# Ten of eleven gate and up pairs of each feed-forward as Strassen groups instead of nine

## The chip, the cores and the metric

The kernel runs on one core of one Trainium2 chip. The metric is device time of one execution in microseconds (us), the median of the runs shown. Lower is better. The core's engines are named as in the profile: PE (TensorE, matmuls), PEld (its weight loads), DVE (VectorE), ACT (ScalarE), POOL (GpSimd) and SP (SyncE, which issues most of the DMAs). Each engine has its own list of instructions and takes them in that order.

## The reference

One encoder block in float32 on 256 rows of width 2048: a SwiGLU feed-forward, two token mixers (band attention and retention) merged by gates, a second SwiGLU feed-forward, and a final norm. Only the two feed-forwards are touched by the change:

```python
D_MODEL = 2048; SEQ = 256; D_FF = 5632
def swiglu_ffn(x, w_gate, w_up, w_down):
    return (jax.nn.silu(x @ w_gate) * (x @ w_up)) @ w_down
...
x = x + 0.5 * swiglu_ffn(rmsnorm(x, norm_ffn1_g[l]), ffn1_w_gate[l], ffn1_w_up[l], ffn1_w_down[l])
... # mixers
x = x + 0.5 * swiglu_ffn(rmsnorm(x, norm_ffn2_g[l]), ffn2_w_gate[l], ffn2_w_up[l], ffn2_w_down[l])
```

`w_gate` and `w_up` are 2048 x 5632, `w_down` is 5632 x 2048. All weights are read from HBM once per use; the 256 rows of activations stay on chip as two tiles of 128 rows (t = 0, 1).

## The kernel before, in words

**Arithmetic.** Float32 precision comes from splitting every operand into a rounded part `hi` and a rest `lo`, and from three products, hi·hi, lo·hi and hi·lo (`three`, lines 132, 133 and 135: activations' hi and lo with the weights' hi, then activations' hi with the weights' lo). Weights arrive in chunks of 256 rows by 512 columns, as a tile of 128 x 1024 elements. Each chunk is split on the chip: ACT writes `hi` (line 123), then DVE writes `lo` = raw - hi (line 124). The products run as matmuls of 128 x 512.

**Steps.** The program is a list of steps, and a step is the work on one split chunk.
- A *standard step* (`standard`) is one chunk of an ordinary matmul job (`Gemm`): 2 k-tiles x 2 row tiles x 3 products = 12 matmuls. Its chunk comes through SP into one of five raw buffers. On DVE it costs one split.
- A *group step* (`Strassen.step`) belongs to a gate and up pair of 512 columns computed as a Strassen group: seven half-size products instead of eight. It has 6 matmuls, on the two row tiles or a combination of them. A group has 28 of them in four phases: phases 0, 1 and 2 have eight each (four "r" steps on a weight block as it is and four "s" steps on a running sum, in pairs "rr", "sr", "sr", "ss"), phase 3 has four "s" steps. Each has a split. DVE also forms the sums of weight blocks: four additions in phase 0 (line 515), eight in phase 1 (lines 570 and 557), all on 128 x 1024 elements. The blocks that stay for the sums (tiles named k and x) come through POOL's queue, and a third block is added to x by four DMAs that accumulate (line 558).
- At the end of a group, DVE has two rescalings (line 745), one combination each at lines 619 and 630, and two splits of the finished product into the operand of `down` (line 364), six instructions on 128 x 512 in all; PE has eight transposes for it (line 369). ACT reads the group's accumulators at the ends of phases (lines 610, 613, 616 and 627). All accumulations of phases 1 to 3 that go on in accumulator "a" wait for that read.

Two numbers make up a group's name in the trace: `z128` is the group that begins at step 128, `loz12833s` is the lo tile of its phase 3, chunk 3, an "s" step. Split tiles of standard steps are plain `hi` and `lo`.

**What runs ahead.** There are four pairs of hi and lo buffers (`SPLIT_BUFS`): before the products of step c are issued, the splits up to step c + 3 are (`prep_upto`), so the split of step c + 4 begins when PE has done with step c.

**The order of a feed-forward.** Of the eleven column blocks of gate and up, nine are Strassen groups and two (`PLAIN`, blocks 9 and 10) are pairs of standard jobs, 8 + 8 standard steps each. `down` is done in seven passes over one or two blocks (`PASSES`), each pass four jobs of 2 standard steps per block; a pass reads x from the residual into the accumulator (line 762) and writes it back (line 765). `weave` puts all standard steps, in the order of a list of jobs, between the group steps. Twelve go first (`LEAD`), the last 14 stay for the end, and the others are dealt out by a credit that grows with each pair of group steps:

```python
job, k = queue[0]
if any(at_hand.get(b, len(steps) + 1) > len(steps) for b in job.needs):
    return False
...
rate = (len(queue) - apart) / (len(groups) * sum(SHARE))
...
    steps.extend(part)
    credit += rate * SHARE[i]
    if i + 1 == len(SHARE):
        at_hand[b] = len(steps) + 7
    turn = i + 1 == 3 * (HALF_K // KC)
    if (turn or credit >= (0.2 if (i + 1) % (HALF_K // KC) == 0 else 0.6)) and next_standard():
        credit -= 1
```

`SHARE` gives 0.85 per pair in phase 0, 1.0 in phase 1, 0.8 and three times 0.4 in phase 2, and 0.15 for each step of phase 3; it sums to 10. A standard step of a `down` pass is only placed once every block that the pass needs is `at_hand`, seven steps after that block's group has ended; until then none is placed, whatever the credit. `turn` asks for one between phases 2 and 3. The lines are those of `weave`; it is called by `ffn`, which the change edits, and by the mixers' projections, which it doesn't touch.

Of the kernel before, what the change touches and what calls it, by code (L numbers as in the profile page):

```python
# [41 lines left out]
HELD = 6  # L42

SHARE = (0.85,) * 4 + (1.0,) * 4 + (0.8,) + (0.4,) * 3 + (0.15,) * 4
PLAIN = (9, 10)
PASSES = ((9, 0), (1, 2), (10, 3), (4, 5), (6,), (7,), (8,))
GATE_WAIT = 5
WARM = (6, 3)
TAIL_PARTS = ((0, slice(0, NB)), (1, slice(0, NB // 2)), (1, slice(NB // 2, NB)))
# [23 lines left out]
def block_kernel(ctx: ExitStack, tc: tile.TileContext, x, g1, w1g, w1u, w1d, gm, w_in, rel, woa, wor, wo,  # L73
# [21 lines left out]
    def tmp_tile(name, tag="t", bufs=None):  # L95
        return tmp.tile([P, NB], F32, tag=tag, name=name, bufs=bufs)
# [9 lines left out]
    def later(n, fn):  # L106
        due.setdefault(state["step"] + n, []).append(fn)
# [529 lines left out]
    def down_done(b, factor, after):  # L637
        def done(acc):
            for t in range(NT):
                xb = xs[t][:, b * NB : (b + 1) * NB]  # L640
                nc.vector.scalar_tensor_tensor(xb, acc[t], factor, xb, op0=ALU.mult, op1=ALU.add)
            if after is not None:
                after(b)

        return done
# [11 lines left out]
    def weave(jobs, apart, groups, lead, start=None):  # L657


        queue = [(job, k) for job in jobs for k in range(0, job.nk, KC)]  # L660
        at_hand = {}

        def next_standard():

            if len(queue) <= apart:
# [4 lines that stand above are left out]
            steps.append(standard(job, k))  # L670
            del queue[0]
            if job.makes is not None and k + KC == job.nk:
                at_hand[job.makes] = len(steps) + 6
            return True

        for _ in range(lead):
            next_standard()
        rate = (len(queue) - apart) / (len(groups) * sum(SHARE))
        credit = 0.0
        first = len(steps) - 8  # L680
        for n, (b, make) in enumerate(groups.items()):
            group = make()
            loads = group.loads()
            if start is not None and n == 0:
                loads[0] = lambda load=loads[0]: [start(), load()]
            kept.extend((first + i if n == 0 else 0, fn) for i, fn in enumerate(loads))
            for i, part in enumerate(group.steps()):
# [8 lines that stand above are left out]
        for job, k in queue:  # L696
            steps.append(standard(job, k))

    def ffn(name, norm, wg, wu, wd, after, start=None):


        nblocks = DFF // NB
        mids, ready = {}, {}

        def put_mid(b, hs):
            mids[b] = Operand(f"{name}a{b}", 1)
            for t in range(NT):
                mids[b].put(0, t, hs[t])

        def plain(b):  # L710
            gates = {}

            wait = GATE_WAIT if start is not None and b == PLAIN[0] else 0

            def gate_done(acc):
                def go():
                    for t in range(NT):
                        gates[t] = tmp_tile(f"{name}g{b}{t}", "gate", 2)
                        nc.scalar.activation(gates[t], acc[t], AF.Silu, scale=norm.scale(t))

                if wait:
                    later(wait, go)
                else:
                    go()

            def up_done(acc):
                for t in range(NT):
                    a = gates[t]
                    nc.vector.scalar_tensor_tensor(a, acc[t], norm.scale(t), a, op0=ALU.mult, op1=ALU.mult)  # L729
                later(4, lambda: put_mid(b, gates))  # L730

            tags = ("acc", "acc")
            up = Gemm(wu, 0, b * NB, D // P, norm, up_done, tags)
            up.makes = b
            return [Gemm(wg, 0, b * NB, D // P, norm, gate_done, ("z", "z") if wait else tags), up]

        def paired(b):
            got = {}

            def evict(t, side, r):  # L740
                if side == 1:
                    nc.scalar.activation(r, r, AF.Silu)
                    got[t] = r
                    return
                nc.vector.scalar_tensor_tensor(got[t], r, norm.scale(t), got[t], op0=ALU.mult, op1=ALU.mult)
                if t == 1:
                    later(4, lambda: put_mid(b, got))

            return Strassen(norm, wu, b * NB, wg, b * NB, evict)

        def down(blocks, last):

            jobs = []

            def act(k, t):
                return mids[blocks[k // 4]](k % 4, t)

            for b in range(D // NB):
                cols = slice(b * NB, (b + 1) * NB)

                def seed(acc, t, cols=cols):
                    nc.scalar.activation(acc, xs[t][:, cols], AF.Copy, scale=2.0)  # L762

                def evict(acc, t, cols=cols):
                    nc.scalar.activation(xs[t][:, cols], acc, AF.Copy, scale=0.5)  # L765

                if last:
                    job = Gemm(wd, 0, b * NB, 4 * len(blocks), act, down_done(b, 0.5, after))
                else:
                    job = Gemm(wd, 0, b * NB, 4 * len(blocks), act, None, ("acc", "acc"), seed)  # L770
                    job.evict = evict
                job.rows = [(m * 4 + i) * P for m in blocks for i in range(4)]
                job.needs = blocks
                jobs.append(job)
            return jobs

        downs = {blocks: down(blocks, blocks is PASSES[-1]) for blocks in PASSES}
        first, second = [plain(b) for b in PLAIN]
        order = [first, second[:1], downs[PASSES[0]], second[1:]] + [downs[p] for p in PASSES[1:]]
        jobs = [job for part in order for job in part]  # L780
        for job, follow in zip(jobs, jobs[1:]):
            job.next = follow
        groups = {b: (lambda b=b: paired(b)) for b in range(nblocks) if b not in PLAIN}
        weave(jobs, len(downs[PASSES[-1]]) * len(PASSES[-1]) * 4 // KC + HELD, groups, LEAD, start)

# [5 lines left out]
    def third_block():  # L791

        there = small.tile([P, NB // P], F32, tag="there", name="there", bufs=1)
        nc.gpsimd.tensor_tensor(there, n1.raw[2][:, 0, : NB // P], mhalf, op=ALU.mult)

    ffn("f1", n1, w1g[0], w1u[0], w1d[0], x_updated(nm), third_block)


# [291 lines left out]
    def tail_done(acc, t, cols):  # L1090
# [24 lines left out]
        for src, dst in ((xs[t][:, c0:c1], slice(c0, c1)), (end, slice(c1, D))):  # L1115
            nc.scalar.activation(src, src, AF.Copy, scale=rs)
            nc.sync.dma_start(out[0, rows, dst], src)
            if dst.start == c0:
                nc.sync.dma_start(out[0, rows, :c0], xs[t][:, :c0])

    ffn("f2", n2, w2g[0], w2u[0], w2d[0], last_block)


# [125 lines left out]
```

## Time and profile before

| | before |
|---|---|
| median of 3 runs | 2069.69 us (2069.14 to 2071.16) |
| profiled execution: its own time | 2071.38 us |
| profiled execution: span of the trace | 2069.5 us |
| PE busy | 2048.4 us (99%), 9256 matmuls |
| PEld busy | 1694.7 us (82%) |
| DVE busy | 1756.4 us (85%), 1825 instructions |
| ACT busy | 1405.0 us (68%), 1734 instructions |
| POOL busy | 273.6 us (13%) |
| moved by DMA | 473.28 MB, mean 229 GB/s |

Starts in the trace count from the span's begin. The first feed-forward fills the first 704 us or so, the second one those from 1377 us on. Matmuls overlap in the pipeline, so the time that one takes from PE is the distance between two starts, not its duration; the same holds for DVE, whose instructions in a row overlap a little. An idle time in brackets stands before the instruction that it precedes, with what ended it.

### The profile page before, as it was taken

The numbers are of one execution on the slowest core, as the hardware profiler recorded it, in microseconds if no ns is written. First come the engines' busy times: TensorE is split into PE (matmuls) and PEld (weight loads), VectorE is DVE, ScalarE is ACT, GpSimd is POOL, SyncE is SP. The second block draws the span as 40 slices with busy tenths as digits, with TensorE's granted clock in tenths as the row PEclk, the third lists the DMA queues.
The fourth block names the chain that finished last, engine by engine and source line by source line (L and its number), as shares of the span: only waits on it lengthen the run. The fifth ranks groups of instructions, "written<-read, shape, count | busy, mean of one in ns | idle before, by whom it ended". The sixth has DMA issues, their size and how long they took to land.

```text
span 2069.5 us, 26149 instructions
## 1 busy us (share of the span) xinstructions
PE 2048.4 (99%) x9256; PEld 1694.7 (82%) x9256; DVE 1756.4 (85%) x1825; ACT 1405.0 (68%) x1734; POOL 273.6 (13%) x322
## 2 busy tenths in 40 slices
PE   9999999999999999999999999999999999999998
PEld 7788888888887888888888888888888888888886
DVE  7998999898997799899966667568989988998986
ACT  8677667777777767776765434556776677677785
POOL 1111211122111110122100000010122012110200
PEclk9999999999999999999999999999999999999999
DMA  8776887788668677898775645575797668876873
GB/s 306 204 227 223 274 227 207 238 264 260 191 230 262 212 205 257 260 289 251 226 268 174 220 134 194 185 238 175 240 275 233 200 224 272 242 206 232 275 214 132
DMA packets 219027, 473.28 MB, mean 229 GB/s; under 512 B 14784, under 2 KB 15536, under 8 KB 218896
## 3 DMA queue, kind: packets, MB, share of 16 engines
q1 hardware_dynamic: 161088, 310.42, 44.7%
q0 software_dynamic: 54752, 155.88, 27.9%
q10 hardware_dynamic: 3056, 5.32, 0.7%
q8 instruction: 72, 1.18, 0.2%
q14 instruction: 59, 0.48, 0.1%
HBM read 462.65 MB, written 8.91 MB: 228 GB/s over the span
## 4 chain that ended last, share of the span: by engine, by line
PE 94%; DVE 2%; DMA 1%; ACT 1%; issue 1%; ACTq 0%; POOLq 0%; POOL 0%; DVEq 0%
PE acc L135 17%; PE acc L132 17%; PE acc L133 17%; DMA raw<-in_ffn_w_down_dram 1%; DVE lo L124 1%; ACT hi L123 1%; PE z684a L135 0%; PE z51a L132 0%; PE z380a L135 0%; PE z51a L133 0%; PE z166a L133 0%; PE z128a L132 0%; PE z380a L132 0%; PE z418a L132 0%; PE z761a L133 0%
## 5 line engine op out<-in xcount | busy, mean ns | idle before, releaser
L124 DVE TENSOR_TENSOR lo<-raw,hi 128x1024 fp32r<-128x1024 f32 (+1 forms) x401 | 487.8, 1220 | 182.1 <-ACT hi L123 177.5
L123 ACT CAST hi<-raw 128x1024 fp32r<-128x1024 f32 (+1 forms) x401 | 418.6, 1048 | 227.9 <-PE acc L133 147.3
L765 ACT ACTIVATE xall<-acc 128x512 f32<-128x512 f32 x96 | 56.6, 589 | 9.6 <-PE acc L135 7.7
L762 ACT ACTIVATE acc<-xall 128x512 f32<-128x512 f32 x96 | 57.5, 599 | 7.5 <-DVE f1g L729 3.1
L132 PE MATMUL acc<-hi,mgh 128*128 128x512 f32 x128 | 50.2, 392 | 0.0
L133 PE MATMUL acc<-hi,mgl 128*128 128x512 f32 x128 | 49.8, 389 | 0.0
L132 PE MATMUL acc<-hi,nma01h 128*128 128x512 f32 x96 | 38.7, 403 | 0.0
L132 PE MATMUL acc<-hi,nma00h 128*128 128x512 f32 x96 | 38.6, 402 | 0.0
L133 PE MATMUL acc<-hi,nma00l 128*128 128x512 f32 x96 | 37.5, 391 | 0.0
L133 PE MATMUL acc<-hi,nma01l 128*128 128x512 f32 x96 | 37.5, 390 | 0.0
L132 PE MATMUL acc<-hi,nma10h 128*128 128x512 f32 x96 | 37.5, 390 | 0.0
L133 PE MATMUL acc<-hi,nma11l 128*128 128x512 f32 x96 | 37.4, 390 | 0.0
L133 PE MATMUL acc<-hi,nma10l 128*128 128x512 f32 x96 | 37.4, 390 | 0.0
L132 PE MATMUL acc<-hi,nma11h 128*128 128x512 f32 x96 | 37.4, 390 | 0.0
L135 PE MATMUL acc<-lo,mgh 128*128 128x512 f32 x128 | 35.6, 390 | 0.0
L135 PE MATMUL acc<-lo,nma00h 128*128 128x512 f32 x96 | 29.6, 390 | 0.0
L135 PE MATMUL acc<-lo,nma11h 128*128 128x512 f32 x96 | 29.6, 390 | 0.0
L135 PE MATMUL acc<-lo,nma01h 128*128 128x512 f32 x96 | 29.6, 390 | 0.0
L135 PE MATMUL acc<-lo,nma10h 128*128 128x512 f32 x96 | 29.6, 390 | 0.0
L135 PEld LDWEIGHTS acc<-lo,mgh 128*128 128x128 f32 x128 | 24.0, 188 | 5.0
L133 PEld LDWEIGHTS acc<-hi,mgl 128*128 128x128 f32 x128 | 24.1, 188 | 4.8
L132 PEld LDWEIGHTS acc<-hi,mgh 128*128 128x128 f32 x128 | 24.0, 188 | 4.9
(6130 smaller groups left out, 6938.3 us busy)
## 6 DMA issues: line engine op xcount, KB each, us to landing
raw<-in_ffn_w_down_dram SPq DMA_DIRECT2D x176, 512.0 KB, 6.0
raw<-in_w_in_dram SPq DMA_DIRECT2D x96, 512.0 KB, 4.7
raw<-in_ffn_w_up_dram SPq DMA_DIRECT2D x32, 512.0 KB, 10.1
raw<-in_w_out_dram SPq DMA_DIRECT2D x32, 512.0 KB, 3.9
raw<-in_ffn_w_gate_dram SPq DMA_DIRECT2D x31, 512.0 KB, 6.0
raw<-in_w_out_att_dram SPq DMA_DIRECT2D x16, 512.0 KB, 4.2
raw<-in_w_out_ret_dram SPq DMA_DIRECT2D x16, 512.0 KB, 4.0
z380x<-in_w_in_dram POOLq DMA_DIRECT2D x8, 512.0 KB, 7.8
```

Source lines behind the costliest of these rows:

```text
L123: nc.scalar.copy(hi[:, p, :], raw[:, p, :])
L124: nc.vector.tensor_sub(lo[:, p, :], raw[:, p, :], hi[:, p, :].bitcast(F32))
L132: nc.tensor.matmul(acc, ahi, whi, start=first, stop=False, **more)
L133: nc.tensor.matmul(acc, alo, whi, start=False, stop=False, **more)
L135: nc.tensor.matmul(acc, ahi, wlo, start=False, stop=last, **more)
L762: nc.scalar.activation(acc, xs[t][:, cols], AF.Copy, scale=2.0)
L765: nc.scalar.activation(xs[t][:, cols], acc, AF.Copy, scale=0.5)
```

## The change

One of the two standard pairs of each feed-forward becomes a Strassen group, so there are ten groups and one standard pair (block 9). The passes of `down` are dealt anew: block 9 alone has the first pass, then come four pairs of blocks, and blocks 8 and 10 have a pass each. The list of standard jobs is now block 9's gate and up, then all passes.

```diff
-PLAIN = (9, 10)
-PASSES = ((9, 0), (1, 2), (10, 3), (4, 5), (6,), (7,), (8,))
+PLAIN = (9,)
+PASSES = ((9,), (0, 1), (2, 3), (4, 5), (6, 7), (8,), (10,))
...
         downs = {blocks: down(blocks, blocks is PASSES[-1]) for blocks in PASSES}
-        first, second = [plain(b) for b in PLAIN]
-        order = [first, second[:1], downs[PASSES[0]], second[1:]] + [downs[p] for p in PASSES[1:]]
+        order = [plain(b) for b in PLAIN] + [downs[p] for p in PASSES]
         jobs = [job for part in order for job in part]
```

By the lists of both programs, counted over both feed-forwards, PE has 48 matmuls of 128 x 512 less; DVE has 24 splits more, 8 more of each of the additions at lines 515, 557 and 570, and 4 small instructions more; ACT has 24 copies at line 123 more and 8 others; SP issues 16 loads less, POOL 24 DMAs more, 8 of them accumulating.

How the order moves is seen on DVE, at the end of the group of block 3 in the first feed-forward and the beginning of the next group (`z128` and `z166` before). A row `lo_...<-raw_...` is the split of a standard step. Before:

```order
L124 TENSOR_TENSOR loz12833s<-z128x_2191,hiz12833s 128x1024
L630 TENSOR_TENSOR z128c_2753<-z128c_2753,z128s_2398 128x512
L124 TENSOR_TENSOR loz16600r<-z166k_2616,hiz16600r 128x1024
L515 TENSOR_TENSOR z166x_2642<-z166x_2642,z166k_2616 128x1024
L124 TENSOR_TENSOR loz16601r<-z166k_2690,hiz16601r 128x1024
L515 TENSOR_TENSOR z166x_2702<-z166x_2702,z166k_2690 128x1024
L124 TENSOR_TENSOR lo_2810<-raw_2598,hi_2809 128x1024
L124 TENSOR_TENSOR loz16600s<-z166x_2642,hiz16600s 128x1024
L745 SCALAR_TENSOR_TENSOR z128c_2753<-z128a,n1rstd,z128c_2753 128x512
L124 TENSOR_TENSOR loz16602r<-z166k_2732,hiz16602r 128x1024
L515 TENSOR_TENSOR z166x_2745<-z166x_2745,z166k_2732 128x1024
L124 TENSOR_TENSOR loz16601s<-z166x_2702,hiz16601s 128x1024
```

After the change the same blocks have the names `z120` and `z152`:

```order
L124 TENSOR_TENSOR loz12033s<-z120x_2051,hiz12033s 128x1024
L124 TENSOR_TENSOR loz15200r<-z152k_2402,hiz15200r 128x1024
L515 TENSOR_TENSOR z152x_2428<-z152x_2428,z152k_2402 128x1024
L630 TENSOR_TENSOR z120c_2511<-z120c_2511,z120s_2250 128x512
L124 TENSOR_TENSOR loz15201r<-z152k_2454,hiz15201r 128x1024
L515 TENSOR_TENSOR z152x_2466<-z152x_2466,z152k_2454 128x1024
L124 TENSOR_TENSOR loz15200s<-z152x_2428,hiz15200s 128x1024
L124 TENSOR_TENSOR loz15202r<-z152k_2478,hiz15202r 128x1024
L515 TENSOR_TENSOR z152x_2490<-z152x_2490,z152k_2478 128x1024
L745 SCALAR_TENSOR_TENSOR z120c_2511<-z120a,n1rstd,z120c_2511 128x512
L124 TENSOR_TENSOR loz15201s<-z152x_2466,hiz15201s 128x1024
L124 TENSOR_TENSOR loz15203r<-z152k_2502,hiz15203r 128x1024
```

The row of the standard step is gone from this place. On DVE's list the longest run of group splits with no standard split among them is 8 before; after the change four runs of 24, 24, 22 and 20 stand in each feed-forward, where a pass of two blocks waits for the second one to be at hand. They run from phase 1 or 2 of the groups of blocks 1, 3, 5 and 7 to the end of phase 0 of the next group. Where the pass is at hand, a standard step follows every pair of group steps until the credit is used up.

On PE the place between phases 2 and 3 of the same group, before:

```order
L133 MATMUL acc_1_2659<-hi_2710,f1a1l_1743 128x512
L135 MATMUL acc_0_2656<-lo_2711,f1a1h_1742 128x512 x2
L135 MATMUL acc_1_2659<-lo_2711,f1a1h_1742 128x512 x2
L132 MATMUL z128a<-hiz12830s,n1a11h 128x512
L133 MATMUL z128a<-hiz12830s,n1a11l 128x512
```

And after the change:

```order
L132 MATMUL z120a<-hiz12023s,n1s7h 128x512
L133 MATMUL z120a<-hiz12023s,n1s7l 128x512
L135 MATMUL z120a<-loz12023s,n1s7h 128x512 x2
L132 MATMUL z120a<-hiz12030s,n1a11h 128x512
L133 MATMUL z120a<-hiz12030s,n1a11l 128x512
```

The standard step between the two phases (accumulators `acc_0`, `acc_1`) has moved away, so phase 3 follows phase 2 directly in the same accumulator `z120a`, which ACT reads in between (line 627).

## The prediction

> **What bounds the kernel now.** I read the busy shares first, then long and short stretches of the feed-forwards, then the distance between starts on PE and DVE, then single waits. The first rows are the page's engine totals and its two costliest groups (count, busy us, mean ns, idle us before).
>
> ```profile
> PE 2048.4 (99%) x9256; PEld 1694.7 (82%) x9256; DVE 1756.4 (85%) x1825; ACT 1405.0 (68%) x1734; POOL 273.6 (13%) x322
> L124 DVE TENSOR_TENSOR lo<-raw,hi 128x1024 fp32r<-128x1024 f32 (+1 forms) x401 | 487.8, 1220 | 182.1 <-ACT hi L123 177.5
> L123 ACT CAST hi<-raw 128x1024 fp32r<-128x1024 f32 (+1 forms) x401 | 418.6, 1048 | 227.9 <-PE acc L133 147.3
> ```
>
> PE is busy throughout, so each matmul removed is worth its distance to the next, if DVE keeps up. The windows by engine (PE, PEld, DVE, ACT, POOL, then clock, DMA share, GB/s) say how near DVE is: the first two hold the middle of the feed-forwards, the others are short ones in the first feed-forward and at the head of the second.
>
> ```profile
> 100.00:625.00 525.00, 524.75 (x2348) 434.10 (x2347) 482.77 (x444) 380.60 (x441) 80.26 (x90) 1.00 0.77 236
> 1450.00:2025.00 575.00, 573.90 (x2567) 475.46 (x2566) 524.38 (x482) 418.58 (x486) 89.20 (x102) 1.00 0.77 236
> 70.00:75.00 5.00, 4.05 (x22) 2.98 (x21) 5.00 (x7) 3.57 (x5) 1.26 (x1) 1.00 0.58 131
> 200.00:225.00 25.00, 24.81 (x110) 20.24 (x109) 25.00 (x23) 17.99 (x22) 5.49 (x6) 1.00 0.83 222
> 1430.00:1455.00 25.00, 25.00 (x115) 20.33 (x114) 25.00 (x25) 16.57 (x18) 7.34 (x8) 1.00 0.84 207
> ```
>
> DVE works 482.8 of 525 us (92%) and 524.4 of 575 us (91%). Its idle time is 42 and 51 us, but not everywhere: in the last three windows it never stops, and in two of them PE loses time. So PE bounds the feed-forwards on average, and DVE does in phase 1 of a group, in places, even with a standard step after nearly every pair.
>
> **Prices.** The timeline of PE shows one group step (309.58 to 310.94) and one standard step (312.30 to 315.02), that of DVE 17 instructions of 128 x 1024 without a pause (203.23 to 222.53), splits and additions mixed.
>
> ```profile
> 309.58 0.39 PE L132 MATMUL z128a<-hiz12822s,n1s7h 128*128 128x512 f32 x1
> 310.94 0.39 PE L132 MATMUL z128a<-hiz12823s,n1s7h 128*128 128x512 f32 x1
> 312.30 0.39 PE L132 MATMUL acc<-hi,f1a1h 128*128 128x512 f32 x1
> 315.02 0.39 PE L132 MATMUL z128a<-hiz12830s,n1a11h 128*128 128x512 f32 x1
> ...
> 203.23 1.22 DVE L124 TENSOR_TENSOR loz8911r<-rawz8911r,hiz8911r 128x1024 fp32r<-128x1024 f32 x1
> 204.36 1.22 DVE L570 TENSOR_TENSOR z89x<-z89x,rawz8911r 128x1024 f32<-128x1024 f32 x1
> ...
> 222.53 1.23 DVE L124 TENSOR_TENSOR lo<-raw,hi 128x1024 fp32r<-128x1024 f32 x1
> ...
> 312.51 0.74 DVE L745 SCALAR_TENSOR_TENSOR z128c<-z128b,n1rstd,z128c 128x512 f32<-128x512 f32 x1
> 316.58 0.69 DVE L630 TENSOR_TENSOR z128c<-z128c,z128s 128x512 f32<-128x512 f32 x1
> 671.49 0.68 DVE L364 TENSOR_TENSOR f1a8l<-f1a8p,f1a8h 128x512 fp32r<-128x512 f32 x1
> 327.26 0.93 PE L369 MATMUL f1a3p<-id_sb,z128c 128*128 128x128 f32 x7
> ```
>
> On PE a standard step takes 2.72 us, a group step 1.36, a matmul 2.72/12 = 0.2267; eight transposes about 0.9. On DVE a split or an addition takes 19.30/17 = 1.135 us, 0.09 less than its duration of 1.22; by the same overlap the small ones take 0.66 (lines 745, 619) and 0.60 (630, 364), so the six that end a group 3 x 0.66 + 3 x 0.60 = 3.8 us.
>
> [...]
>
> **Removed from PE.** 48 matmuls: 48 x 0.2267 = 10.9 us, 5.44 in each feed-forward. All of it counts where PE bounds. The 16 SP loads that go lay beside PE's work (PE 524.75 of 525 us busy at a DMA share of 0.77), so I count nothing for them.
>
> **Added to DVE.** Per feed-forward 12 splits and 12 additions, 24 x 1.135 = 27.2 us, and two small ones, about 1 us. Against an idle time of 51 us in the second window less the 5.4 that PE gives up this still fits, on average, so the total alone costs nothing. The same holds for ACT (12 copies of 1.05 us against 156 us idle) and POOL (12 DMAs more on a queue that is 16% busy).
>
> **Moved.** What doesn't fit is the order. A pair of group steps gives PE 2.72 us of work, and DVE 2.27 us in phases 2 and 3, 3.40 in phase 0 and 4.54 in phase 1; a standard step adds 2.72 to PE and 1.135 to DVE. Without standard steps DVE falls behind; with one per pair in phases 2 and 3 it gets ahead, but by no more than the four split buffers hold. I sum PE work less DVE work over each place where standard steps fail to come, from the order in the section on the change, per feed-forward:
>
> - Run of 24 after block 1: 24 x 1.36 + 0.9 = 33.5 for PE; 24 splits, 8 additions and 3.8 make 40.1 for DVE: -6.6. The stretch of phase 1 ahead of it (4 group steps, 1 standard) has 8.2 against 9 x 1.135 = 10.2: -2.1. Together -8.7.
> - Run of 24 after block 3: -6.6; ahead of it phase 0 with two standard steps -0.6 (17.2 against 17.8) and half of phase 1 with two -0.5 (10.9 against 11.4): -7.7.
> - Run of 22 after block 5: 30.8 against 28 x 1.135 + 3.8 = 35.6: -4.8; ahead of it 6 group and 2 standard steps, 13.6 against 14 x 1.135 = 15.9: -2.3. Together -7.1.
> - Run of 20 after block 7: 28.1 against 24 x 1.135 + 3.8 = 31.0: -2.9; ahead of it phase 0 with two standard steps -0.6 and phase 1 with three -2.5 (19.0 against 19 x 1.135 = 21.6). Together -6.0.
> - The first group's phase 1: one standard step is left of three. 8 x 1.36 + 2.72 = 13.6 against 17 x 1.135 + 2 x 0.66 = 20.6: -7.0. Before it was 19.0 against 22.9: -3.9.
>
> PE stalls by what such a sum exceeds the lead that DVE has at its beginning. The lead is not in the trace as a number. From the code: the copy of step c + 4 starts when PE has done c; copy and split take 1.05 + 1.22 us, while PE has three steps and the four hi matmuls of the next, 4.08 + 0.91 = 5.0 us. So with group steps in the buffers DVE is 2.7 us ahead at best in time of need, and never more than four steps, 5.4 us. The trace bounds it from two sides: the window 1430 to 1455 holds the second feed-forward's -3.9 with PE at 25.00, so a lead of 3.9 was there, with standard steps in the buffers; and here a sum of about 1.9 (phase 1 of block 2's group up to its fourth standard step: 20.8 against 22.7) already made PE wait:
>
> ```profile
> 223.81 0.73 PE L135 MATMUL acc<-lo,f1a0h 128*128 128x512 f32 x2 [0.19 <-DVE lo L124]
> ```
>
> I take 2.7 for the four runs, which are all group steps: 6.0 + 5.0 + 4.4 + 3.3 = 18.7 us. For the head I take the 3.9 that the second feed-forward showed: 3.1 there. In the first one DVE had no lead (window 70 to 75: DVE 5.00, PE 4.05), so all of the difference counts, 3.1, and a standard step missing in phase 0, 2.72 - 1.135 = 1.6: 4.7.
>
> **The seams.** Where no standard step lies between phases 2 and 3, PE waits for ACT's read of the accumulator:
>
> ```profile
> 312.50 0.69 ACT L627 ACTIVATE z128c<-z128a,n1minus 128x512 f32<-128x512 f32 x1 [0.40 <-PE z128a L135]
> ```
>
> It ends at 313.19, and the next matmul could have begun at 312.30: 0.9 us, at four groups per feed-forward. At those places DVE is already behind, and a PE that waits lets it catch up; I count 0 and keep 8 x 0.9 = 7.2 for the upper bound.
>
> **The sum.** -10.9 + (18.7 + 4.7) + (18.7 + 3.1) = +34.3 us. The profiled execution took 2071.4 us (span 2069.5), so 2105.7 for it; the median of the runs is 1.7 lower: **2104 us**. Bounds for the median: a lead of 5.4 everywhere leaves 3.3 + 2.3 + 1.7 + 0.6 per feed-forward and 1.6 + 4.7 at the heads, +11 us: 2081. No lead at all gives 29.5 per feed-forward, heads as above, seams in full, +63: 2133.
>
> **Rivals.**
> - *The lag stays hidden; faster.* If the buffers carried 8.7 us, the largest run would pass and only the matmuls would count: 2069.7 - 10.9 = 2059. For it: DVE's total fits, and -3.9 passed without loss. Against it: four steps of 1.36 us are 5.4 us, and the window 200 to 225. From a lead of about 6.9 us on the sign would turn (1.8, 0.8 and 0.2 left of the runs of a feed-forward, 4.7 and 0.1 at the heads: 10.4 against 10.9). Chance 9%.
> - *Little change.* A lead near 5.4 us and a first head that absorbs its loss: 2064 to 2078, of which a third is within 0.2% (4.1 us, about what a measurement of this kernel can tell from no change) and the lowest part below it. Chance 12%.
> - *The clock falls.* The end of the first feed-forward has a single wait of 2.2 us on PE, and right after it a window at half clock:
>
> ```profile
> 671.63 0.66 PE L369 MATMUL f1a8p<-id_sb,z320c 128*128 128x128 f32 x4 [2.22 <-DVE gains L280]
> 672.40:675.70 3.30, 3.30 (x9) 2.60 (x8) 0.69 (x1) 0.51 (x1) 0.00 (x0) 0.50 0.98 374
> ```
>
>  If each of the eight runs did that for 3.3 us, as here, and lost half of it, 1.7 us each, the time would be 2104 + 14 = 2118. Against it: the stall of a run comes in pieces, and from 70 to 75 PE lost 0.95 of 5 us at a clock of 1.00. Chance 9%. [...]
> - *Loads come late.* With no standard steps a group's eight blocks through POOL's queue must land in less time. For one group they took 9.6 and 12.7 us in the median, and by the order on DVE the last is needed some eleven instructions, 12.5 us, after its buffer is free:
>
> ```profile
> z418x<-in_w_in_dram POOLq DMA_DIRECT2D x8, 512.0 KB, 9.6
> z418k<-in_w_in_dram POOLq DMA_DIRECT2D x4, 512.0 KB, 12.7
> ```
>
>  Two us more in each of eight runs: 2120. Chance 10%.
>
> The forecast has the remaining 60%, with 2081 to 2133 as its own range. The range given, 2075 to 2134, takes in the last two rivals and a part of "little change". Faster 11% (the first rival and 2% of the second), same 4%, slower 85%.
>
> **What would show it.** PE has 9208 matmuls, and the mean distance inside a step stays 0.227. DVE in the middle of the feed-forwards goes from 92% to 95% or more, and PE's waits on DVE's lo and ACT's hi appear in phase 0 of the groups of blocks 2, 4, 6 and 8, 3 to 6 us each, with the clock at 1.00. The mixers' part, between, takes as long as before. I would be wrong if those places showed no waits, if waits there were on DMAs, or if PE also waited in phases with a standard step per pair.

## The result, and the profile after

The changed kernel takes **2141.1 us** (median of 4 runs, 2134.4 to 2144.9) against 2070.4 in the same session: ratio 1.034, 95% interval 1.0319 to 1.0362. The direction was as forecast, the size was not: +71 us instead of +34, and 2141 lies above the range, which ended at 2134. The profiled execution took 2137.6 us, with a span of 2135.8 (before 2071.4 and 2069.5).

The engine totals of the changed kernel and its costliest group on DVE, from the page:

```profile
PE 2072.5 (97%) x9208; PEld 1681.4 (79%) x9208; DVE 1811.8 (85%) x1877; ACT 1424.8 (67%) x1766; POOL 294.8 (14%) x346
L124 DVE TENSOR_TENSOR lo<-raw,hi 128x1024 fp32r<-128x1024 f32 (+1 forms) x369 | 448.6, 1219 | 196.8 <-ACT hi L123 196.1
```

PE has its 48 matmuls less, but its busy time is 24 us longer (a matmul shows 0.39 us and the next one starts 0.23 us behind it; where PE waits, the rest of the 0.39 no longer lies under the next one) and its idle time 42 (span less busy: 63.3 against 21.1). DVE works 55 us more at the same price per split (1.219 us, 1.220 before). The windows, columns as before (PE, PEld, DVE, ACT, POOL, clock, DMA share, GB/s), of the changed kernel; the last but one lies between the feed-forwards, the last is at half clock:

```profile
100.00:625.00 525.00, 506.77 (x2209) 405.18 (x2208) 478.98 (x442) 370.20 (x433) 87.02 (x98) 1.00 0.76 232
1450.00:2025.00 575.00, 553.04 (x2391) 441.88 (x2390) 519.07 (x479) 398.34 (x463) 98.37 (x112) 0.99 0.76 230
70.00:75.00 5.00, 3.79 (x15) 2.47 (x14) 5.00 (x6) 2.25 (x3) 1.26 (x1) 1.00 0.64 137
850.00:1400.00 550.00, 547.24 (x2537) 454.95 (x2537) 415.71 (x526) 319.97 (x403) 48.26 (x58) 1.00 0.70 219
1748.00:1751.20 3.20, 3.20 (x9) 2.53 (x8) 2.77 (x3) 2.30 (x4) 1.45 (x2) 0.50 1.04 385
```

In the feed-forwards PE falls from 524.75 to 506.77 us of 525, while DVE's share does not rise as forecast, to 95%: it is 91% and 90%. Two engines that wait for each other by turns, neither of them full. The stretch between the feed-forwards is as busy as it was (PE 547 of 550).

Four single waits on PE, from its timeline (start, us, instruction, idle time before it and what ended it): the seam between phases 2 and 3, the transposes that wait for DVE's last operation of a group, a standard step in a phase 1 that has four of them for its four pairs, and a standard step of down in phase 2 behind a run; the last row is ACT's, just ahead of it:

```profile
163.84 0.50 PE L132 MATMUL z48a<-hiz4830s,n1a11h 128*128 128x512 f32 x1 [0.91 <-ACT z48c L627]
177.06 0.63 PE L369 MATMUL f1a1p<-id_sb,z48c 128*128 128x128 f32 x4 [0.72 <-DVE z48c L745]
202.16 0.74 PE L135 MATMUL acc<-lo,f1a1h 128*128 128x512 f32 x2 [0.41 <-DVE lo L124]
1746.06 0.50 PE L132 MATMUL acc<-hi,f2a3h 128*128 128x512 f32 x1 [1.60 <-ACT hi L123]
1744.97 1.04 ACT L123 CAST hi<-raw 128x1024 fp32r<-128x1024 f32 x1 [2.85 <-DMA raw<-in_ffn_w_down_dram]
```

The wait of 1.60 us is not ACT's fault: ACT itself waited there for a chunk of down's weights. The chunks' median time to land rose, by the page's DMA issues of before and of after, and behind them the wait of ACT on them in the changed kernel (before it was 27 us in all):

```profile
raw<-in_ffn_w_down_dram SPq DMA_DIRECT2D x176, 512.0 KB, 6.0
```
```profile
raw<-in_ffn_w_down_dram SPq DMA_DIRECT2D x176, 512.0 KB, 7.0
```
```profile
ACT hi L123 <- DMA raw<-in_ffn_w_down_dram: 45.7, 29, 4.2
```

To see all of it in one place, I took from each trace the distance between the starts of neighbouring PE instructions, less 0.227 us per matmul (0.109 per transpose), and gave what was over (from 0.02 us on) to the group and phase of the instruction ahead. Microseconds of both feed-forwards; "head" is the first group of each, the phases are those of all other groups (waits in standard steps between them included):

| kernel | time | head | phase 0 | phase 1 | phase 2, with the seam |
|---|---|---|---|---|---|
| before | 2070 | 3.2 | 1.5 | 0.6 | 2.9 |
| changed | 2141 | 11.0 | 24.0 | 15.0 | 30.6 |
| e1 changed, no additions | 2110 | 8.4 | 5.8 | 13.5 | 28.4 |
| e2 ten groups, even | 2115 | 11.9 | 18.2 | 27.4 | 3.5 |
| e9 ten, even, no additions | 2082 | 8.4 | 1.6 | 15.5 | 3.4 |
| e13 ten, even, more in phase 1 | 2094 | 15.2 | 21.8 | 2.6 | 1.9 |
| e14 nine, thin | 2091 | 2.2 | 8.0 | 18.5 | 0.3 |
| e15 nine, two runs | 2096 | 3.2 | 9.7 | 6.1 | 12.9 |
| e5 changed, seam moved | 2133 | 10.9 | 34.5 | 18.2 | 12.5 |

### The profile page after: what moved, and what is told of

The parts are those of the page before. It is cut to its first block, busy times and chain, and to the rows that moved or that the text cites. A ratio compares the mean times of both kernels' runs of the same rounds, so it can differ in the third digit from the quotient of the medians.

```text
span 2135.8 us, 26160 instructions
## 1 busy us (share of the span) xinstructions
PE 2072.5 (97%) x9208; PEld 1681.4 (79%) x9208; DVE 1811.8 (85%) x1877; ACT 1424.8 (67%) x1766; POOL 294.8 (14%) x346
## 5 line engine op out<-in xcount | busy, mean ns | idle before, releaser
L124 DVE TENSOR_TENSOR lo<-raw,hi 128x1024 fp32r<-128x1024 f32 (+1 forms) x369 | 448.6, 1219 | 196.8 <-ACT hi L123 196.1
L123 ACT CAST hi<-raw 128x1024 fp32r<-128x1024 f32 (+1 forms) x369 | 385.1, 1048 | 236.5 <-PE acc L133 146.9
L133 PE MATMUL acc<-hi,nma11l 128*128 128x512 f32 x96 | 37.4, 390 | 0.0
L132 PE MATMUL acc<-hi,nma11h 128*128 128x512 f32 x96 | 37.4, 390 | 0.0
L133 PE MATMUL acc<-hi,nma10l 128*128 128x512 f32 x96 | 37.4, 390 | 0.0
```

The lines of the kernel that those rows point to most:

```text
L123: nc.scalar.copy(hi[:, p, :], raw[:, p, :])
L124: nc.vector.tensor_sub(lo[:, p, :], raw[:, p, :], hi[:, p, :].bitcast(F32))
L132: nc.tensor.matmul(acc, ahi, whi, start=first, stop=False, **more)
L133: nc.tensor.matmul(acc, alo, whi, start=False, stop=False, **more)
```

## The experiments

Times before in these sessions were 2069 to 2071 us. Ratios are to the kernel before, with the 95% interval.

**e1: the additions of phase 0 left out.** Line 515 of the changed kernel does nothing; the order stays.

```
         def first(self, jc):
-            nc.vector.tensor_add(self.x[jc], self.x[jc], self.kept[jc])
+            pass
```

> The changed kernel with the four additions of phase 0 (line 515, x + k) left out of every group; the products are then of other sums, all loads, splits and matmuls stay as they are. Theory A (DVE falls behind in the runs without standard steps): each run's deficit shrinks by 4 x 1.135 = 4.5 us, so the waits in phase 0 of the groups of blocks 2, 4, 6 and 8 go (1.7 to 3.1 us each in the trace) and with them most of what follows in phase 1; 30 to 40 us less than the changed kernel, 2100 to 2112. Theory B (the loads of the stretch after a run come late, and the clock falls): DVE is not the cause, the loss stays, 2130 or more.

2109.9 us (2106.6 to 2111.0), ratio 1.0189 (1.0174 to 1.0204): 31 us less for 100 additions (113 us of DVE work; 20 of them lie in the mixers). Phase 0, where they stood, drops from 24.0 to 5.8; phase 1 and the late loads of phase 2 stay. DVE's work is a cause; half of the loss isn't touched by it.

**e2: the same ten groups without runs.** Each pass of down has one block only, so its steps come free earlier and the longest run is 8.

```
-PASSES = ((9,), (0, 1), (2, 3), (4, 5), (6, 7), (8,), (10,))
+PASSES = ((9,), (0,), (1,), (2,), (3,), (4,), (5,), (6,), (7,), (8,), (10,))
```

> The changed kernel with eleven passes of down over one block each, so that a pass never waits for a second block: the longest run of group splits without a standard one falls from 24 to 8, with the same ten groups and the same additions and splits. It costs 4 passes x 8 x (0.53 + 0.48) = 32 us of ACT more per feed-forward. Theory A (the order): the runs' losses go, 45 to 60 us less than the changed kernel, 2080 to 2096. Theory C (the amount of DVE work: 24 instructions more per feed-forward can't be hidden wherever they stand): 2125 or more. Theory B (late loads behind a run): as A, since no run is left, but with the clock at 1.00 throughout.

2115.0 us (2112.1 to 2119.1), ratio 1.0212 (1.0195 to 1.0229). It lies between the ranges of both theories. This is the run on which the prediction's reason fails. Without any run 45 of the 71 us remain. The seams' waits and the waits behind late chunks are gone (phase 2: 30.6 to 3.5), but now phase 1 of every group waits for DVE, and so does phase 0 of two groups in three, a standard step per pair or not:

```profile
214.16 0.73 PE L135 MATMUL z84a<-loz8413s,n1s6h 128*128 128x512 f32 x2 [0.61 <-DVE loz8413s L124]
216.43 0.73 PE L135 MATMUL acc<-lo,f1a1h 128*128 128x512 f32 x2 [0.61 <-DVE lo L124]
```

The two phases are not alike. Single passes also give ACT 62 us more to do (busy 1486.9 us against 1424.8; from 100 to 625 us 405.6 against 370.2), since each job of down reads the residual and writes it back (lines 762 and 765). In the 9 us ahead of the 12 groups, of 18, that lose 0.8 us or more in phase 0, DVE sits idle for 0.9 to 1.9 us at a stretch, in most of them right behind such reads and writes on ACT; ahead of the six that lose 0.2 us or less, for some 0.5 at most (DVE ahead of block 2's group, then PE in its phase 0):

```profile
175.22 1.23 DVE L124 TENSOR_TENSOR loz4833s<-z48x,hiz4833s 128x1024 fp32r<-128x1024 f32 x1 [1.82 <-ACT hiz4833s L123]
182.79 0.73 PE L135 MATMUL z84c<-loz8400s,n1s5h 128*128 128x512 f32 x2 [0.55 <-DVE loz8400s L124]
```

So part of phase 0's 18.2 us may come with ACT's added work and not with the thin mix alone; that was not tried by itself.

**e3: a shorter lead in the second feed-forward**, so that eight standard steps more are left to be dealt out; the first one is the control.

```
-        weave(jobs, ..., groups, LEAD, start)
+        weave(jobs, ..., groups, LEAD if start is not None else 4, start)
```

> The changed kernel with 4 instead of 12 standard steps ahead of the first group in the second feed-forward alone; eight more are left to be dealt out, so that the longest run there is 14 instead of 24, then 12, 8, 8. The first feed-forward is untouched and is the control. Theory A: the second feed-forward loses 10 to 20 us instead of 42, 2115 to 2125 in all. Theory C: it stays, 2135 to 2145.

2118.7 us (2116.3 to 2124.5), ratio 1.0238 (1.0222 to 1.0255). The second feed-forward's loss falls from 42.0 to 23.2 us by the same reckoning, the first's stays at 45. In the same window as above PE rises from 553.04 to:

```profile
1450.00:2025.00 575.00, 562.74 (x2479) 455.72 (x2478) 529.21 (x488) 409.92 (x476) 97.21 (x111) 1.00 0.76 234
```

Eight standard steps in reach are worth 22 us. Longest run 14 instead of 24, and more standard steps per pair: both parts gain, so this run doesn't tell them apart.

**e4: nine groups with passes like the changed kernel's.** `PASSES = ((9,), (0, 1), (10, 2), (3, 4), (5, 6), (7,), (8,))` in the kernel before.

> The kernel before (nine groups, two standard pairs) with block 9 given a pass of its own and the other passes dealt anew, (0, 1), (10, 2), (3, 4), (5, 6), (7), (8): the part of the change without the tenth group. The longest run stays 8. Theory A and C: as the kernel before, 2067 to 2075. If a pass of its own for block 9 or the new pairs cost anything by themselves: over 2080.

2068.6 us (2066.8 to 2072.2), ratio 0.9997 (0.9988 to 1.0006). The new dealing of the passes costs nothing with nine groups; it is the tenth group.

**e5: the seam.** In phase 2 the order of steps is changed so that a residual step lies last and ACT's read of the accumulator is over when phase 3 begins.

```
+                if phase == 2:
+                    order = [r[0], r[1], s[0], r[2], s[1], s[2], s[3], r[3]]
```

> The changed kernel with the last r step of phase 2 moved behind the last s step, so that six matmuls on another accumulator lie between phase 2's last use of accumulator a and phase 3's first, where ACT reads it. Eight waits of PE on line 627 of 0.8 to 0.9 us stand in the changed kernel's trace. Theory D (the seam is a wait of its own): 6 to 8 us less than the changed kernel. My prediction's view (at that place DVE is behind anyway and would make PE wait a little later): within 2 us of it.

2133.4 us (2130.3 to 2136.3), ratio 1.0299 (1.0283 to 1.0316). That is some 8 us less than the changed kernel: theory D's range, and not the prediction's view, which had the seams at 0. Phase 2 loses 18 us less, phase 0 10.5 and phase 1 3 more: more than half of what PE doesn't wait in phase 2 it waits for DVE one phase later, as the prediction argued. The 18 are not the seams alone: PE's waits on ACT's hi of standard steps fall from 8.9 to 0.3 us, and the mean granted clock is 0.998 against 0.995.

**e6: the next group's block loads later**, meant to go out from twelve steps before the group on instead of when a buffer is free, out of the way of down's weights.

```
-            kept.extend((first + i if n == 0 else 0, fn) ...)
+            kept.extend((first + i if n == 0 else len(steps) - 12, fn) ...)
```

> The changed kernel with the eight loads of a group's blocks (line 526) held back until 12 steps before the group begins; in the changed kernel five of them go out right behind the accumulating loads, some 30 us before they are needed, while raw chunks of standard steps land 11 to 17 us after their issue and the clock halves three times behind the waits on them. Theory B (late raw chunks behind a run): 10 to 18 us less than the changed kernel, no fall of the clock in the second feed-forward. If the raw chunks are late whoever loads beside them: within 4 us of it. If the blocks come too late now: slower, with waits of ACT on tiles named k in phase 0.

2136.0 us (2135.2 to 2141.4), ratio 1.0318 (1.03 to 1.0335). The second feed-forward's three falls of the clock are gone (mean granted clock 0.998 against 0.995), but the waits behind late chunks stay: PE's waits on ACT's hi are 8.4 us against 8.9. The run says little of the block loads, because the edit hardly moved them: measured from the group's first matmul they go out within some 2 us of where they did, in all groups of both feed-forwards. At the group of block 3 in the first one, whose first matmul starts at 247.3 us in the changed kernel and at 247.6 here, the first of them (the changed kernel, then this one):

```profile
207.91 1.23 POOL L526 DMA_DIRECT2D z120k<-in_ffn_w_up_dram  x1
```
```profile
207.11 1.23 POOL L526 DMA_DIRECT2D z120k<-in_ffn_w_up_dram  x1
```

In both kernels five of them go out there within 5 us, among chunks of down's weights, and the DMA engines are full (the changed kernel; DMA share 1.04):

```profile
200.00:230.00 30.00, 28.02 (x120) 22.00 (x119) 22.43 (x20) 18.76 (x23) 8.70 (x11) 1.00 1.04 315
```

So it stays open whether the block loads make down's chunks late. Late chunks alone don't make PE wait: the kernel before has 61 of 176 that take over 10 us to land, the changed kernel 71, and PE's waits on ACT's hi are 1.2 us in all before. In e2, without runs, those waits are 2.0 us, so they come with the runs. How a run turns late chunks into waits, whether by holding their buffers or by the transfers that crowd behind it, wasn't tried by itself.

**e7: phase 0's additions on POOL** (`nc.gpsimd.tensor_add` at line 515).

> The changed kernel with phase 0's additions (line 515) on POOL instead of DVE. Theory A and C (DVE's work is the cause): as with these additions left out, 25 to 35 us less than the changed kernel, if POOL's addition takes under 2.5 us; less of it, or a loss, if POOL takes longer or slows DVE beside it.

2244.7 us (2233.6 to 2246.4), ratio 1.0819 (1.0787 to 1.085), far off what was hoped. An addition takes 3.0 us on POOL in the mean (2.3 to 5.4), 1.22 on DVE, and beside it DVE's own splits take longer (the costliest group on POOL and the splits on DVE of this run, then the splits of the changed kernel; mean ns behind the busy time):

```profile
L515 POOL TENSOR_TENSOR z908x<-z908x,z908k 128x1024 f32<-128x1024 f32 x4 | 14.8, 3730 | 3.6 <-DMA z908x<-in_ffn_w_gate_dram 3.6
...
L124 DVE TENSOR_TENSOR lo<-raw,hi 128x1024 fp32r<-128x1024 f32 x367 | 504.7, 1379 | 208.3 <-ACT hi L123 207.3
```
```profile
L124 DVE TENSOR_TENSOR lo<-raw,hi 128x1024 fp32r<-128x1024 f32 x367 | 447.3, 1222 | 196.8 <-ACT hi L123 196.1
```

**e8: e3, e5, e6 and e7 together.**

> The changed kernel with the r step last in phase 2, the later block loads, phase 0's additions on POOL, and 4 steps ahead of the first group in the second feed-forward. If the causes are the ones named and add up: 71 us less 7, 14, 30 and 22 is 2070 or below, about the kernel before. If one makes another worse: 2085 or more.

2210.3 us (2208.9 to 2212.5), ratio 1.0672 (1.0656 to 1.0688). POOL's part outweighs the others, so it says nothing on them; e11 leaves it out.

**e9: e2 without the additions of phase 0**, i.e. the edits of e1 and e2.

> Ten groups per feed-forward with eleven passes of one block (no run of more than eight group steps, 2115.0 us in its own run), and the addition of the kept block to the other in phase 0 (line 515) left out, so the kernel computes other sums: 100 additions less on DVE. Theory M (what is left of the loss is DVE's amount: one standard step per pair no longer reaches, because each group brings more DVE work than the standard steps beside it give time for): 2070 to 2090 us, PE's waits on DVE's lo down from about 32 us to under 10, most of what remains in phase 1. Theory O (what is left comes from the order or from transfers, not from DVE): above 2100 us, waits nearly as before. From the run without the addition under the changed order, 2110 against 2141, 31 us is what the additions were worth there.

2082.4 us (2081.2 to 2084.6), ratio 1.0056 (1.0042 to 1.007). Theory M's range. Phase 0 goes from 18.2 to 1.6, phase 1 from 27.4 to 15.5. ACT's added work is the same as in e2, so what e2 still lost hangs on DVE's work.

**e10: nine groups in runs.** The kernel before, four groups' blocks due later (runs of 28, 26 and 21).

```
-                    at_hand[b] = len(steps) + 7
+                    at_hand[b] = len(steps) + {0: 27, 2: 43, 3: 31, 5: 43}.get(b, 7)
```

> The kernel before with its nine groups and its amount of DVE work, but four groups' due times moved later so that the standard steps come to an end and group steps run without one: three runs of 28, 26 and 21 per feed-forward, where the changed kernel has 24, 24, 22 and 20. It completes the square: nine groups even 2069 to 2070, ten groups even 2115, ten groups in runs 2141. Theory P (the runs themselves, as in the prediction: each sum of about 7 to 9 us less a lead of 2.7): six runs x 4 to 6 = 24 to 36 us, 2094 to 2106. Theory M (the amount decides, runs cost only where DVE has nothing spare): under 2082. Between, both have a part. If the cost of runs adds to that of the amount as between the two kernels of ten groups (26 us for eight runs): six runs x 3.3 = 20, 2090.

2127.2 us (2125.6 to 2134.2), ratio 1.0278 (1.0261 to 1.0294): more than any theory said. These runs go past the seam between phases 0 and 1, and there PE waits for ACT's read of a sum, 15.3 us of idle time in six places, with a fall of the clock behind four of them (granted clock 0.99 from 100 to 625 us and from 1450 to 2025, 1.00 in both before; one wait on PE, and the window that follows, at 0.50):

```profile
330.19 0.80 PE L132 MATMUL z160c<-hiz16010r,n1s3h 128*128 128x512 f32 x1 [2.79 <-ACT z160s L613]
```
```profile
330.20:333.50 3.30, 3.30 (x8) 2.63 (x9) 3.30 (x4) 1.93 (x2) 0.00 (x0) 0.50 0.52 166
```

The changed kernel's runs end before that seam. The run is thus no fair copy of them; e15 is.

**e11: e3, e5 and e6 together.**

> The changed kernel with three edits that were each run alone: the last residual step of phase 2 put at its end (-7.6), the loads for the next group twelve steps later (-5.1) and LEAD 4 in the second feed-forward (-22.4). If they add up: 2141 - 35 = 2106 us. If the seam's gain is taken by DVE where DVE is late anyway: 2110 to 2120. Under 2100 if the transfers were what the other two still waited for. Either way above the kernel before: no order of these steps makes up for the DVE work, by theory M.

2120.1 us (2119.2 to 2124.0), ratio 1.0241 (1.0227 to 1.0255). They don't add up: it is e3's 2118.7 again (e6's edit hardly moves the loads, so that these are e3 and e5). In the first feed-forward the seam's gain comes back as waits in phase 0 (3.1, 2.8, 2.4 and 1.7 us behind the four runs became 4.3, 3.9, 3.3 and 2.9).

**e12: one line of the kernel before**, the load of the mixer's gain ten jobs earlier.

```
-    at(mix - 14, lambda: later(4, load_gain(gm, 1)))
+    at(mix - 24, lambda: later(4, load_gain(gm, 1)))
```

> The kernel before with one line changed: the load of the mixer's gain ten jobs earlier (24 instead of 14 ahead of the mixer's start). It has nothing to do with the change; it takes away the one wait of 2.2 us at the end of the first feed-forward, behind which the clock stands at 0.50 for 3.4 us. If the fall comes from the wait: 2.2 + 1.7 us less, about 2066, clock 1.00 from 672 to 676. If the fall comes from something else there (the transposes or the DMA share of 0.98): 2067.5 and the half clock stays.

2065.7 us (2064.8 to 2067.0, 9 runs), ratio 0.9978 (0.9968 to 0.9988): faster than both kernels. The wait of 2.2 us is gone, and so is the fall behind it:

```profile
672.00:676.00 4.00, 4.00 (x19) 3.30 (x18) 1.51 (x2) 2.50 (x4) 0.00 (x0) 1.00 0.84 301
```

**e13: e2 with the standard steps dealt out otherwise.** Their number and DVE's work stay.

```
+FFN_SHARE = (1.0,) * 4 + (1.45,) * 4 + (0.3,) + (0.0,) * 7
...
+        share = FFN_SHARE if lead == LEAD else SHARE
-                credit += rate * SHARE[i]
+                credit += rate * share[i]
```

> Ten groups with eleven passes of one block, as in the run that gave 2115.0, and the feed-forward's standard steps dealt out otherwise over a group's phases, their number the same: about 38 instead of 28 per feed-forward after phase 1's 40 pairs, about 15 instead of 24 after phase 2's (SHARE of its own for the feed-forward). Theory M (a phase is short where its own standard steps are too few, phase 1 above all: 8 x 1.36 + 2.8 x 2.72 = 18.5 us of PE against 16 x 1.135 + 2.8 x 1.135 + 1.3 = 22.6 of DVE; with 3.8 of them 21.2 against 23.8): 2095 to 2105 us. Theory T (the total decides, wherever the standard steps lie): 2112 to 2118. Theory L (it isn't DVE but something every group does, such as loads): no change from 2115.

2094.5 us (2093.3 to 2095.7), ratio 1.0124 (1.0106 to 1.0142). Half a microsecond below theory M's range, far from the others'. Phase 1, which got the steps, falls from 27.4 to 2.6 us; phase 0, which got one more per feed-forward, doesn't gain (18.2 and 21.8): ten of its groups have ACT's four reads and writes of the residual right ahead, and lose 1.6 to 2.0 us each. DVE does more in the same window at an equal total (e2, then e13):

```profile
100.00:625.00 525.00, 512.50 (x2245) 412.44 (x2244) 485.76 (x448) 405.61 (x499) 86.99 (x98) 1.00 0.76 233
```
```profile
100.00:625.00 525.00, 519.34 (x2306) 425.31 (x2305) 496.79 (x459) 416.89 (x509) 87.41 (x99) 1.00 0.76 235
```

**e14: nine groups, thin.** The kernel before with fewer standard steps beside the groups, 0.78 per unit of `SHARE` as with ten, the others ahead of and behind them.

```
-LEAD = 12
+LEAD = 28
-HELD = 6
+HELD = 14
-PASSES = ((9, 0), (1, 2), (10, 3), (4, 5), (6,), (7,), (8,))
+PASSES = ((9,), (10,), (0, 1), (2, 3), (4, 5), (6,), (7,), (8,))
-        order = [first, second[:1], downs[PASSES[0]], second[1:]] + [downs[p] for p in PASSES[1:]]
+        order = [plain(b) for b in PLAIN] + [downs[p] for p in PASSES]
-        first = len(steps) - 8
+        first = len(steps) - 8 - (16 if lead == LEAD else 0)
```

> Nine groups, both plain pairs first, LEAD 28 and HELD 14: of the standard steps 24 more per feed-forward lie ahead of and behind the groups, so that 0.78 instead of 1.04 are dealt per unit of SHARE, as with ten groups, evenly, with no run over eight. DVE's total is that of the kernel before (2070). Theory M (what costs is how few standard steps lie beside a group's phases 0 and 1): 18 groups x about 1.5 to 2.2 us as the ten-group kernel in this order lost, 2095 to 2110 us. Theory T (DVE's total): 2069 to 2076.

2090.7 us (2089.7 to 2091.4), ratio 1.0104 (1.0086 to 1.0122): 4 us below theory M's range, far above T's. It also lost the wait on the mixer's gain, some 4 us by e12, so that the thin mix costs about 25. DVE's total is the kernel before's (1758 us), and phases 0 and 1 lose 26.5 instead of 2.1.

**e15: nine groups, with runs in the changed kernel's places.** `{2: 39, 5: 41}` instead of e10's numbers: two runs of 24 per feed-forward, from phase 1 to the end of the next group's phase 0.

> Nine groups, the kernel before with two due times per feed-forward moved later: two runs of 24 group steps each, from the second step of phase 1 to the end of the next group's phase 0, where the changed kernel has its first runs, and none that crosses from phase 0 into phase 1 as those of the run with 2127 us did (there ACT's read at line 613 alone cost 16 us). Theory P (the sums of the prediction: 33.5 against about 40, and 2 ahead, less a lead of 2.7, 4 to 6 us for each of four runs, 0.9 for each of four seams): 2088 to 2098 us. Theory A (as between the two kernels of ten groups, 26 us for eight runs): 2083. Theory N (with the nine groups' total, runs cost nothing): under 2076.

2095.6 us (2093.7 to 2096.4), ratio 1.0127 (1.0111 to 1.0143): +26.5 for four runs, 6.6 each, in theory P's range. Runs alone cost what the prediction said, seams included.

## Why the prediction was wrong

The square, in us over the kernel before: nine groups in runs +26 (e15, four runs), ten groups even +45 (e2), ten groups in runs +71. The forecast had a price for the runs and nothing for the second.

Point by point, from the profiled executions:

| term of the sum | forecast | measured |
|---|---|---|
| 48 matmuls | -10.9 | 9208 matmuls at the same distance (a standard step takes 2.72 us, 1738.86 to 1741.58): -10.9 |
| runs, first feed-forward (phase 2 of the group to phase 0 of the next; the first and the fourth with the phase 1 ahead, as in their sums) | 6.0, 5.0, 4.4, 3.3 | 7.1, 4.9, 3.6, 3.6 |
| runs, second | the same | 6.5, 5.1, 3.6, 3.7 |
| heads | 4.7 and 3.1 | 4.6 and 3.2 |
| phase 1 behind each run (7.0) and of the last groups | 0 | 8.8 |
| phase 0 of the second group of each | 0 | 3.3 |
| phase 2 behind a run: chunks that land late, and the clock | 0 | 18.8, about 16 more than before |

The terms that were worked out came near: 38.1 us for the runs against 37.4, nearly in the order of size that the sums gave, and the heads within 0.2, though 1.7 and 1.8 us of the heads' loss lie in phase 2, behind the place that was summed. The seams' 0.9 are in the measured runs. The last three rows, for which the forecast had nothing, come to 28; of the whole difference of 66 us between the two profiled executions 3 are not placed, and the median of the runs is another 3.5 above its profile.

**The step that failed** is "this still fits, on average, so the total alone costs nothing", with "what doesn't fit is the order": all places beside the runs and the heads were put at nothing. The runs showed 45 us for ten groups without a run (e2), about 25 for nine groups with the old total and the thin mix (e14), and in the changed kernel itself the 28 us of the last three rows. The sum of PE work less DVE work was made beside the runs alone. Made for phase 1 of an even order with ten groups it would have said so: 3.0 standard steps (27 for the 36 pairs of nine groups, the first group left out) give PE 8 x 1.36 + 3.0 x 2.72 = 19.0 us, DVE 16 x 1.135 + 3.0 x 1.135 + 1.3 = 22.9: a lack of 3.8, 1.1 more than the lead of 2.7. Measured in e2: 27.4/18 = 1.5 per group. With 4.0, as in the kernel before and in e13, the lack is 2.2, less than the lead, and phase 1 loses 0.6 and 2.6 us in all. Behind a run the lead is used up, and there phase 1 loses 0.9 us even with four, in each of eight places. Phase 0 is another matter: by the prediction's sum it lacks only 0.6 with two standard steps, so its 18.2 us in e2 don't follow from this sum (see e2).

The bookkeeping for a feed-forward shows how much was lost: the change gives up 16 standard steps, each with 2.72 - 1.135 = 1.6 us to spare for DVE (25), and adds a group of 39.0 us on PE and 40 x 1.135 + 3.8 = 49.2 on DVE (10). Of DVE's 51 us to spare 36 go (the prediction's own figures, 27.2 + 1 + 5.4, come to 34). The 15 that are left are an average; DVE can bank only 2.7 of them at a time, by the prediction's estimate. In the changed kernel's order the runs hold the standard steps back and hand them over behind, where phases 1 then have one per pair. That, and the part of e2's loss that may be ACT's, would fit that eight runs (at e15's 6.6 each, 53 us) and the thin mix (45) come to 71 together and not to 98.

The prediction had a row that said it: phase 1 of block 2's group already waited, at a sum of about 1.9, with a standard step per pair. It was used as a bound for the lead, and not as a place that would lose more. Its test, "or if PE also waited in phases with a standard step per pair", came out against it (202.16 above).

**Loads and clock** stood among the rivals, as another way in which it could go. They came in addition: the late chunks were down's weights on SP's queue, not the groups' blocks on POOL's, and they hit behind the runs, not in them. Most of phase 2's extra 16 us hang on them: some 10 us of PE's loss were waits on ACT that had its chunk late (2.0 before), some 6 were half clock (four falls of 3.41 us, in which matmuls start 0.43 us apart instead of 0.23, 1.6 us of loss each; one fall before). They are not a loss of their own in full: in e5 nearly all of them are gone (PE's waits on ACT's hi 0.3 us, clock 0.998), and the seams' waits too, and the time fell by 8 us only, because PE then waited for DVE. What makes PE wait for these chunks stays open (e6).

**Other readings.** DVE at 95% or more: wrong, 91 and 90%; it waits for ACT (196.1 us ahead of lo), which waits for PE's buffers (146.9 us ahead of hi). Waits in phase 0 behind the runs: there, 1.7 to 3.1 instead of 3 to 6, as a part lies at the seam. The mixers: as before. *The lag stays hidden* and *little change*: refuted by e15, nine groups with DVE's old total lose 6.6 per run.

What is not settled: phases 0 and 1 lose 45.6 us in e2 and 26.5 in e14, both at 0.78. Two groups more account for 3 (26.5/16 each). By the order on PE the groups that are counted have 3.0 standard steps in phase 1 in both, and in phase 0 21 for nine groups in e2 against 20 for eight: 0.17 steps per group x 1.6 us x 18 groups, some 5. The other 11 us or so I can't place; ACT's added work in e2 is the nearest candidate, untried.

## What to carry to other kernels

Where two kinds of work are interleaved because one is short of PE time and the other has it to spare, a change that turns the second kind into the first costs twice: the lack grows and the filler shrinks. Sum both engines phase by phase with the filler that is left there, against what the buffers can bank, and not over the whole stage: 91% on average hid a loss of 3% here. And when a step is found short in the profile before, ask first what the change does to that place.

Once the mix is thin, where the filler lies matters as much as how much there is: the same steps moved from phase 2 to phase 1 gave 21 us back (e13); a wait taken away upstream of the short engine gave back less than half (e5, e11).

## What the runs showed of the hardware

- POOL: an addition of 128 x 1024 fp32 takes 3.0 us in the mean, and DVE's splits beside it rise from 1.222 to 1.379 us in the mean (e7). Moving DVE's work there lost on both here: 2244.7 us against 2141.1.
- In the changed kernel the granted clock falls to 0.50 four times, for 3.41 us each, at 703.43, 1747.91, 1877.61 and 2007.32 us (and once more at the end of the span, from 2130.20 on, where PE is idle); these starts are 1044.48, 129.71 and 129.71 us apart, which are 306, 38 and 38 times 3.413. Ahead of them PE had waits of 2.21, 1.60, 1.47 and 1.82 us, and in the 3.41 us before each fall it worked for 1.23, 1.78, 1.88 and 1.59 us. The length of the wait doesn't decide by itself: one of 1.50 us, from 223.54 to 225.04, brought no fall (clock 1.00 from 219 to 232), nor did one of 2.05 us in e10, from 130.48 to 132.53 (1.00 from 132.50 to 136.00). The waits on PE, two of the changed kernel and one of e10:

```profile
1875.95 0.50 PE L132 MATMUL acc<-hi,f2a5h 128*128 128x512 f32 x1 [1.47 <-ACT hi L123]
225.04 0.50 PE L132 MATMUL acc<-hi,f1a1h 128*128 128x512 f32 x1 [1.50 <-ACT hi L123]
```
```profile
132.53 0.50 PE L132 MATMUL z51c<-hiz5110r,n1s3h 128*128 128x512 f32 x1 [2.05 <-ACT z51s L613]
```

- A matmul behind a wait showed 0.50 us instead of 0.39 (163.84, 1746.06), and the next one started 0.34 us behind it instead of 0.23 (164.18, 1746.40), so these waits cost some 0.1 us more than the time by which they put off the start.
